# Moving the split activations of a decoder trunk to other byte addresses in SBUF

## The chip, the cores and the metric

The kernel runs on one core of one Trainium2 chip. The metric is the device time of one execution in microseconds. Two timed runs of the kernel before took 1018.0 and 1018.07 us, median 1018.04.

A core has a matrix engine (PE in the profile, with its weight loads shown apart as PEld), a vector engine (DVE), a scalar engine (ACT), a general engine (POOL) and SP, whose queue issues most of the transfers from main memory. Data sits in SBUF, 128 partitions with a byte address along each; products are summed in PSUM, in banks.

## The reference, cut to what matters

A decoder trunk of two layers, 256 positions by 1024 channels, float32. Each layer is a feed-forward block, a token mixer with memory cross-attention beside it, and a second feed-forward block, each added to the residual:

```python
def rms_norm(x, g):
    y = x * lax.rsqrt(jnp.mean(x * x, axis=-1, keepdims=True) + EPS)
    return y * g

def swiglu(x, w_in, w_out):
    gate, up = jnp.split(x @ w_in, 2, axis=-1)
    return (jax.nn.silu(gate) * up) @ w_out

for i in range(2):
    x = x + 0.5 * swiglu(rms_norm(x, ffn1_norm_g[i]), ffn1_w_in[i], ffn1_w_out[i])
    x = x + mixer(rms_norm(x, mix_norm_g[i])) @ w_out      # layer 0: mLSTM, layer 1: windowed attention
    x = x + 0.5 * swiglu(rms_norm(x, ffn2_norm_g[i]), ffn2_w_in[i], ffn2_w_out[i])
```

The hidden width of the feed-forward blocks is 2816. The four feed-forward blocks hold most of the multiplications.

## The kernel before, in words

**Split products.** Every large product is made three times in a rounded float32 format (fp32r). A value is split into a high part (rounded) and a low part (what the rounding left), and the sum high·high + high·low + low·high stands for the full product. `mm3` (L224 to L228) issues these three products: L225 is weights-high by x-high, L226 weights-high by x-low, L227 weights-low by x-high. Each has a stationary operand of 128 by 128, loaded by a weight load of its own, and a moving operand of 128 partitions by 256 columns.

**Weights.** `wtile` (L216) brings a weight tile of 128 by 1024 to the buffer `wr` over SP's queue, and `split` (L204) makes `wh` on ACT (L211) and `wl` on DVE (L212). There are 5, 8 and 8 buffers of these.

**The normed residual.** An object of the class `Norm` stands for each point at which the residual is normed: x0 before the first feed-forward block, x1 before the mLSTM mixer, x2 and x3 before the second and third feed-forward blocks, x4 before the attention mixer, x5 before the last feed-forward block. Its method `put` takes one chunk of the residual at a time (256 channels, `[128, 2, 256]`, four chunks in all), scales it by the norm's gain and splits it (`split_gain`, L239): the high part `xh` by ACT (recorded at L132), the low part `xl` by DVE (L241). The factor of each position (one over the root mean square) is not in there: `chain` (L293) works it out beside the products that already run, with small matrix products on a column of ones (L231) and, a little later, on the identity (also L231, `bcast_rows`), and it is applied to the results.

**A feed-forward block.** `ffn_in` (L471) makes 11 groups of 256 gate and 256 up columns. Each group takes 2 halves of the channels, 2 parts (gate, up), 2 blocks of 128 columns and 4 chunks of 128 channels, three products each: 96. So there are 11 x 96 = 1056 products to a block, in which `xh` or `xl` is the moving operand and `wh` or `wl` the stationary one. The second half of `ffn` (L509) makes the output from the hidden values, which lie in buffers `u`: 22 x 8 x 3 = 528 products with `u` moving. The first product on the last of the four residual chunks is the 55th of a block.

**The mixers.** Some groups of a mixer also have `xh`, `xl` moving; those whose result has positions in rows (`rows=True`) have them stationary and the weights moving. Between these groups stand short products for heads, written in by a planner (`Weave`) with due times.

**Order.** PE and SP run in the order in which the program is written; semaphores are placed by the framework, from what each instruction reads and writes. Tiles come from pools, each with a number of buffers; the pools lie in SBUF in the order in which they are opened (L110 to L125), one behind the other, so the order and the sizes of the pools set the addresses.

**Addresses before.** Taken from the program: `xh` (4 buffers of 2048 bytes) from byte 28608, `xl` from 36800, `u` (31 buffers) from 44992, `v` (2 buffers of 2064 bytes, 2080 apart) from 108480, `wr` from 112640, `wh` from 133120, `wl` from 165888. Counted modulo 512, every `xh`, `xl` and `u` begins at 448, every `wr`, `wh` and `wl` at 0.

Of the kernel before, what the change touches and what calls it, by code (L numbers as in the profile page):

```python
# [11 lines left out]
F32R = mybir.dt.float32r  # L12
# [7 lines left out]
P = 128  # L20
T = 256
# [27 lines left out]
G_MEM, G_F1, G_MIX, G_F2, G_XQ, G_XK, G_AH, G_BQ, G_BK, G_END = 0, 8, 24, 40, 56, 58, 60, 68, 69, 70  # L49
# [6 lines left out]


WARM = 18


class Weave:
# [37 lines left out]
def tile_trunk(ctx: ExitStack, tc: tile.TileContext, a, out):  # L99
# [3 lines left out]
    def mk(pool, shape, dt, tag):  # L103
        seq[0] += 1
        return pool.tile(shape, dt, tag=tag, name=f"{tag}_{seq[0]}")

    def pool(name, bufs, **kw):
        return ctx.enter_context(tc.tile_pool(name=name, bufs=bufs, **kw))

    cst = pool("cst", 1)  # L110
    wv = Weave()


    xhp = pool("xhp", 4)
    xlp = pool("xlp", 4)
    up = pool("up", 31)
    vp = pool("vp", 2)
    wrp = pool("wrp", 5)
    whp = pool("whp", 8)
    wlp = pool("wlp", 8)  # L120
    tp = pool("tp", 7)
    sp = pool("sp", 2)
    ap1 = pool("ap1", 1)
    gp = pool("gp", 1)
    cp = pool("cp", 24)  # L125
# [24 lines left out]
    def mo():  # L150
        return mk(pb8, [P, 512], F32, "bank")
# [47 lines left out]
    def g(i):  # L199
        return gcol[:, i:i + 1]  # L200
# [38 lines left out]
    def split_gain(src, gc, hi, lo):  # L239
        act(hi, src, AF.Copy, scale=gc)  # L240
        nc.vector.scalar_tensor_tensor(out=lo, in0=src, scalar=gc, in1=hi.bitcast(F32),  # L241
                                       op0=ALU.mult, op1=ALU.subtract)
# [18 lines left out]
    class Norm:  # L261


        def __init__(self, gi, rows=True, half=True):
            self.gi, self.rows, self.half, self.rc = gi, rows, half, None
            self.done = False
            self.xT, self.xh, self.xl = [], [], []

        def put(self, xn):
            c2 = len(self.xT)  # L270
            hi, lo = mk(xhp, [P, 2, T], F32R, "xh"), mk(xlp, [P, 2, T], F32R, "xl")
            for m in range(2):
                split_gain(xn[:, m], g(self.gi + 2 * c2 + m), hi[:, m], lo[:, m])
            self.xh.append(hi)
            self.xl.append(lo)
            self.xT.append(xn)
            self.square(xn, c2 == 0)
            if c2 == 3:
                self.fold()
# [115 lines left out]

    kT = [mk(cst, [P, 2, T], F32, f"kT{i}") for i in range(2)]
    vM = mk(cst, [P, 2, 512], F32, "vM")
    x0 = Norm(G_F1)

    def memory():  # L400

# [2 lines left out]
        bank = mo()  # L404
        for i in range(WARM):
            nc.tensor.matmul(bank, idle[:, :P], idle, start=True, stop=True, skip_group_check=True)
# [565 lines left out]

    def program():
        yield from memory()
        x1, x2, x3 = Norm(G_MIX, half=False), Norm(G_F2), Norm(G_F1 + 8)
        x4, x5 = Norm(G_MIX + 8, rows=False), Norm(G_F2 + 8)
        yield from ffn(x0, a["ffn1_w_in"][0], a["ffn1_w_out"][0], x1, late_constants)
        yield from mixer_a(x1, x2)
        yield from ffn(x2, a["ffn2_w_in"][0], a["ffn2_w_out"][0], x3)
        yield from ffn(x3, a["ffn1_w_in"][1], a["ffn1_w_out"][1], x4, rope_tables)  # L980
        yield from mixer_b(x4, x5)
        yield from ffn(x5, a["ffn2_w_in"][1], a["ffn2_w_out"][1])

    with tc.manual_schedule(engines={mybir.EngineType.PE, mybir.EngineType.SP}):
        wv.run(program())
# [38 lines left out]
```

## Time and profile before

| | us |
|---|---|
| median of the two timed runs | 1018.04 |
| the profiled execution | 1018.06 |
| its span, first to last instruction | 1016.3 |
| PE busy | 1007.1 (99%) |
| DVE busy | 656.8 (65%) |
| ACT busy | 520.5 (51%) |

1.8 us of the profiled execution lie outside the span. A product's duration in the trace overlaps the next one's, so the pace of PE is read from the distance between two starts, not from the durations; where a window is asked for, a product counts if any part of it lies inside.

### The profile page before, as it was taken

How to read it: one execution, taken by the hardware profiler on the slowest of the kernel's cores; microseconds unless marked ns; L12 is line 12 of the kernel's file. 1: busy time of each engine (PE TensorE's matmuls, PEld its weight loads, DVE VectorE, ACT ScalarE, POOL GpSimd, SP SyncE). 2: the span in 40 equal slices, each digit the busy share in tenths (PEclk: the TensorE clock that was granted, in tenths of full speed). 3: DMA queues.
4: the chain of work that ended last, by engine and by line, in shares of the span. 5: the costliest groups of instructions: out<-in, count | busy, mean ns of one | idle time of the engine just before them, and what ended most of it. 6: DMA issues, size and time to landing. Idle time of an engine off the chain costs nothing.

```text
span 1016.3 us, 20689 instructions
## 1 busy us (share of the span) xinstructions
PE 1007.1 (99%) x8626; PEld 987.5 (97%) x8626; DVE 656.8 (65%) x1063; ACT 520.5 (51%) x764; POOL 35.5 (3%) x32
## 2 busy tenths in 40 slices
PE   8999999999999999999999999999999999999998
PEld 7999999999999999999999999999978899999998
DVE  6866665567756766665667666555786666665551
ACT  7754545446556644444545444544565654444440
POOL 1200000000000000000000000000211000000000
PEclk9999999999999999999999999999999999999999
DMA  9776655666544476655666666566531256665650
GB/s 311 240 248 194 191 187 182 191 189 180 170 146 145 153 221 192 201 178 187 197 200 195 192 200 190 173 192 204 180 104 63 65 160 214 198 195 179 189 173 21
DMA packets 173204, 182.70 MB, mean 180 GB/s; under 512 B 7124, under 2 KB 168328, under 8 KB 173112
## 3 DMA queue, kind: packets, MB, share of 16 engines
q1 hardware_dynamic: 171872, 179.60, 56.9%
q10 hardware_dynamic: 1016, 1.58, 0.4%
q8 instruction: 67, 1.10, 0.4%
q0 software_dynamic: 224, 0.22, 0.2%
q14 instruction: 25, 0.20, 0.1%
HBM read 180.32 MB, written 1.05 MB: 178 GB/s over the span
## 4 chain that ended last, share of the span: by engine, by line
PE 97%; DVE 1%; DMA 1%; POOL 0%; SPq 0%; ACT 0%; issue 0%
PE bank L225 30%; PE bank L226 30%; PE bank L227 30%; PE bank L231 5%; PE bank L236 1%; DMA wr<-in_mem_w_kv_dram 1%; DVE wl L212 0%; PE bank L921 0%; POOL col L379 0%; DVE col L591 0%; SPq L410 0%; ACT wh L211 0%; DVE u L596 0%; ACT u L132 0%; SPq L218 0%
## 5 line engine op out<-in xcount | busy, mean ns | idle before, releaser
L212 DVE TENSOR_TENSOR wl<-wr,wh 128x1024 fp32r<-128x1024 f32 (+1 forms) x347 | 414.7, 1197 | 280.9 <-ACT wh L211 280.3
L211 ACT CAST wh<-wr 128x1024 fp32r<-128x1024 f32 (+1 forms) x347 | 356.9, 1031 | 396.8 <-PE bank L226 370.7
L225 PE MATMUL bank<-xh,wh 128*128 128x256 f32 x1544 | 429.5, 278 | 0.0
L227 PE MATMUL bank<-xh,wl 128*128 128x256 f32 x1544 | 427.3, 277 | 0.0
L226 PE MATMUL bank<-xl,wh 128*128 128x256 f32 x1544 | 427.3, 277 | 0.0
L226 PEld LDWEIGHTS bank<-xl,wh 128*128 128x128 f32 x1544 | 290.3, 188 | 0.1
L225 PEld LDWEIGHTS bank<-xh,wh 128*128 128x128 f32 x1544 | 290.0, 188 | 0.1
L227 PEld LDWEIGHTS bank<-xh,wl 128*128 128x128 f32 x1544 | 289.9, 188 | 0.0
L225 PE MATMUL bank<-u,wh 128*128 128x256 f32 x896 | 249.2, 278 | 0.0
L227 PE MATMUL bank<-u,wl 128*128 128x256 f32 x896 | 247.9, 277 | 0.0
L226 PE MATMUL bank<-u,wh 128*128 128x256 f32 x896 | 247.9, 277 | 0.0
L225 PEld LDWEIGHTS bank<-u,wh 128*128 128x128 f32 x896 | 168.3, 188 | 0.7 <-issue 0.7
L226 PEld LDWEIGHTS bank<-u,wh 128*128 128x128 f32 x896 | 168.3, 188 | 0.1
L227 PEld LDWEIGHTS bank<-u,wl 128*128 128x128 f32 x896 | 168.3, 188 | 0.0
L225 PE MATMUL bank<-wh,xh 128*128 128x256 f32 x208 | 60.0, 288 | 0.0
L226 PE MATMUL bank<-wl,xh 128*128 128x256 f32 x208 | 58.0, 279 | 0.0
L227 PE MATMUL bank<-wh,xl 128*128 128x256 f32 x208 | 57.9, 278 | 0.0
L476 DVE TENSOR_TENSOR t<-bank,rb 128x256 f32<-128x256 f32 x88 | 36.6, 421 | 7.2 <-PE bank L227 7.2
L225 PEld LDWEIGHTS bank<-wh,xh 128*128 128x128 f32 x208 | 39.1, 188 | 0.5 <-issue 0.3
L226 PEld LDWEIGHTS bank<-wl,xh 128*128 128x128 f32 x208 | 39.1, 188 | 0.1
L227 PEld LDWEIGHTS bank<-wh,xl 128*128 128x128 f32 x208 | 39.0, 188 | 0.0
L479 DVE TENSOR_TENSOR t<-t,bank 128x256 f32<-128x256 f32 x88 | 32.8, 413 | 1.8 <-ACT t L132 1.8
(169 smaller groups left out, 676.0 us busy)
## 6 DMA issues: line engine op xcount, KB each, us to landing
wr<-in_ffn_w_in_dram SPq DMA_DIRECT2D x176, 512.0 KB, 3.7
wr<-in_ffn_w_out_dram SPq DMA_DIRECT2D x80, 512.0 KB, 3.5
wr<-in_a_w_in_dram SPq DMA_DIRECT2D x28, 512.0 KB, 3.7
wr<-in_b_w_in_dram SPq DMA_DIRECT2D x14, 512.0 KB, 4.6
wr<-in_a_w_out_dram SPq DMA_DIRECT2D x12, 512.0 KB, 3.3
wr<-in_b_w_out_dram SPq DMA_DIRECT2D x12, 512.0 KB, 3.3
wr<-in_ffn_w_out_dram SPq DMA_DIRECT2D x16, 256.0 KB, 2.6
wr<-in_mem_w_kv_dram SPq DMA_DIRECT2D x7, 512.0 KB, 8.1
```

What stands on the lines that cost most here:

```text
L211: last[0] = nc.scalar.copy(hi[:, i * n:(i + 1) * n], src[:, i * n:(i + 1) * n])
L212: tt(out=lo[:, i * n:(i + 1) * n], in0=src[:, i * n:(i + 1) * n], in1=hi[:, i * n:(i + 1) * n].bitcast(F32), op=ALU.subtract)
L225: nc.tensor.matmul(ps, wh, xh, start=start, stop=False, skip_group_check=True)
L226: nc.tensor.matmul(ps, wh, xl, start=False, stop=False, skip_group_check=True)
L227: nc.tensor.matmul(ps, wl, xh, start=False, stop=stop, skip_group_check=True)
L231: nc.tensor.matmul(ps, lhsT, rhs, start=start, stop=stop, skip_group_check=True)
L236: nc.tensor.transpose(ps, src, ident[:k, :k])
L476: tt(out=t[:, m], in0=ps[m][:, :T], in1=x.rb, op=ALU.mult)
L479: tt(out=t[:, m], in0=t[:, m], in1=ps[m][:, T:], op=ALU.mult)
```

## The change

The two pools of `xh` and `xl` go. In their place is one pool `xsp` with one buffer of 16 x 256 float32 plus 80: all eight pieces of a `Norm` (four high, then four low) are slices of one tile `xs`. Each `Norm` has an offset `at`, in float32, at which its slices begin: 64 for the two mixers, and 68, 76, 52 and 60 for x0, x2, x3 and x5. The pools `vp` and `sp` are opened earlier, so they move in SBUF too. No instruction is added or taken away by the text of the change, and no product, copy or transfer has another size.

```diff
+XPAD = 80
...
-    xhp = pool("xhp", 4)
-    xlp = pool("xlp", 4)
+    vp = pool("vp", 2)
+
     up = pool("up", 31)
-    vp = pool("vp", 2)
+    sp = pool("sp", 2)
+    xsp = pool("xsp", 1)
     wrp = pool("wrp", 5)
     whp = pool("whp", 8)
     wlp = pool("wlp", 8)
     tp = pool("tp", 7)
-    sp = pool("sp", 2)
...
-        def __init__(self, gi, rows=True, half=True):
-            self.gi, self.rows, self.half, self.rc = gi, rows, half, None
+        def __init__(self, gi, rows=True, half=True, at=64):
+
+            self.gi, self.rows, self.half, self.rc, self.at = gi, rows, half, None, at
...
         def put(self, xn):
             c2 = len(self.xT)
-            hi, lo = mk(xhp, [P, 2, T], F32R, "xh"), mk(xlp, [P, 2, T], F32R, "xl")
+            if c2 == 0:
+                self.tile = mk(xsp, [P, 16 * T + XPAD], F32R, "xs")
+            hi, lo = (self.tile[:, c0:c0 + 2 * T].rearrange("p (m t) -> p m t", m=2)
+                      for c0 in (self.at + 2 * c2 * T, self.at + (8 + 2 * c2) * T))
...
-    x0 = Norm(G_F1)
+    x0 = Norm(G_F1, at=68)
...
-        x1, x2, x3 = Norm(G_MIX, half=False), Norm(G_F2), Norm(G_F1 + 8)
-        x4, x5 = Norm(G_MIX + 8, rows=False), Norm(G_F2 + 8)
+        x1, x2, x3 = Norm(G_MIX, half=False), Norm(G_F2, at=76), Norm(G_F1 + 8, at=52)
+        x4, x5 = Norm(G_MIX + 8, rows=False), Norm(G_F2 + 8, at=60)
```

The change names the phases 464, 496, 400 and 432 in place of 448. That is the position of a slice modulo 512, counted from the position of the weights: 68 is four float32, 16 bytes, behind 64, and so on for +48, -48 and -16 bytes.

## The prediction

> **What bounds the kernel now.** I read the page first, then the pace of PE by windows, then the places where that pace differs. On the page I look at the span, the busy shares, the granted clock and the chain that ended last; of the groups, the three with `xh` or `xl` moving.
>
> ```profile
> span 1016.3 us, 20689 instructions
> ...
> PE 1007.1 (99%) x8626; PEld 987.5 (97%) x8626; DVE 656.8 (65%) x1063; ACT 520.5 (51%) x764; POOL 35.5 (3%) x32
> ...
> PEclk9999999999999999999999999999999999999999
> ...
> PE 97%; DVE 1%; DMA 1%; POOL 0%; SPq 0%; ACT 0%; issue 0%
> ...
> L225 PE MATMUL bank<-xh,wh 128*128 128x256 f32 x1544 | 429.5, 278 | 0.0
> L227 PE MATMUL bank<-xh,wl 128*128 128x256 f32 x1544 | 427.3, 277 | 0.0
> L226 PE MATMUL bank<-xl,wh 128*128 128x256 f32 x1544 | 427.3, 277 | 0.0
> ```
>
> PE is busy for 99% of the span at full clock, and the chain is PE for 97%. No transfer and no other engine is late. So the time is the number of products times their pace, and only the pace, or a new wait on PE, can move it. Of the 3 x 1544 products with x moving, 4 x 1056 = 4224 are in the feed-forward blocks.
>
> The pace, from windows of PE alone (columns: window, its length, busy time with the number of products that touch it, clock, DMA share, GB/s):
>
> ```profile
> 60.00:150.00 90.00, 90.00 (x796) 1.00 0.62 192
> ...
> 375.00:465.00 90.00, 90.00 (x797) 1.00 0.61 191
> 475.00:525.00 50.00, 50.00 (x444) 1.00 0.63 198
> 555.00:645.00 90.00, 90.00 (x797) 1.00 0.63 192
> 655.00:705.00 50.00, 50.00 (x443) 1.00 0.65 197
> 855.00:945.00 90.00, 90.00 (x797) 1.00 0.62 191
> ```
>
> A product that begins up to 0.28 us ahead of a window counts in it, so the pace is (90 + 0.28)/797 = 113.3 ns with x moving, in each block, and (50 + 0.28)/443 or 444 = 113.2 to 113.5 ns with `u` moving. It is one pace for three operand tiles. But there is a second one. At the start of each stage two short groups break the stream: the products on a column of ones and, some microseconds later, those on the identity. The first rows are of the chain of work in order of time (start, length, what), the others of PE in order of time.
>
> ```profile
> 45.81 0.34 PE bank L231 x4
> ...
> 54.73 0.45 PE bank L231 x4
> ...
> 538.36 0.34 PE bank L231 x4
> ...
> 544.46 0.44 PE bank L231 x4
> ...
> 224.03 0.36 PE L225 MATMUL bank<-xh,wh 128*128 128x256 f32 x1
> 224.23 0.28 PE L226 MATMUL bank<-xl,wh 128*128 128x256 f32 x1
> 224.35 0.28 PE L227 MATMUL bank<-xh,wl 128*128 128x256 f32 x1
> ...
> 229.65 0.28 PE L227 MATMUL bank<-xh,wl 128*128 128x256 f32 x1
> 229.77 0.61 PE L231 MATMUL bank<-con,rc 128*128 128x128 f32 x4
> ```
>
> Here 224.35 to 229.65 is 15 rounds of three products: 5.30/45 = 117.8 ns. After the identity products the pace is 113.3 again, with the same tiles at the same addresses. So **PE has two paces, 113.3 and 117.8 ns**, and what sets which one holds, here, is how the stream was last broken. The slow spell lasts 6.1 us in a block (538.36 to 544.46) and 8.9 in the first; three of one and one of the other are 27 us, about 230 of the 4224 products.
>
> The weight load is the nearest limit below. Where a product has one moving column, only loads are left to pace PE:
>
> ```profile
> 223.56 0.53 PEld L231 LDWEIGHTS bank<-ones,acc 128*128 128x128 f32 x4
> 224.00 0.19 PEld L225 LDWEIGHTS bank<-xh,wh 128*128 128x128 f32 x1
> ...
> 357.44 0.52 PEld L231 LDWEIGHTS bank<-ones,acc 128*128 128x128 f32 x4
> 357.89 0.19 PEld L225 LDWEIGHTS bank<-xh,wh 128*128 128x128 f32 x1
> ```
>
> Four loads take 0.44 and 0.45 us from the first start to the next one behind them: 0.89/8 = 111.2 ns. The steady pace is 2.1 ns over that. Loads stay as they are in the feed-forward blocks: there x is the moving operand.
>
> **The change part by part.** *Addresses, by adding pool sizes.* `v` begins at 28608 and takes 2 x 2080, so `u` begins at 32768, which is 0 modulo 512; `sp` takes 4864 bytes, `xs` begins at 101120 and `wr` at 117824, which is 64. With `at` = 64 a mixer's slices begin at 101376, 0 modulo 512: against the weights they lie where they lay, 448 to 0 before and 0 to 64 now, and so does `u`. The four blocks are 16, 48, -48 and -16 bytes off that. So the only products that read from a new place relative to the rest are the 4224; no part of it has a row in this trace, since every x, u and weight slice of before begins at a multiple of 64 bytes.
>
> *What a moving operand off a multiple of 64 costs.* The nearest row is `v`, whose two buffers lie 2080 bytes apart, so every second head reads it 32 bytes off. It moves 257 columns in full float32, two records a product; the first row is of the buffer at a multiple of 64, the second of the other:
>
> ```profile
> 299.55 1.46 PE L231 MATMUL bank<-v,u 128*128 128x257 f32 x6
> ...
> 306.51 1.46 PE L231 MATMUL bank<-v,u 128*128 128x257 f32 x6
> ```
>
> Six records take 1.46 us at both places. At two decimals that is a difference under 0.01/6 = 1.7 ns a record; it is no fp32r stream, which is twice as dense, so it speaks for nothing but doesn't settle it. Bounds for one fp32r product: from below, 111.2 ns, the load alone, -2.1; from above the other pace that the trace shows, 117.8, +4.5. I take 0, because the three operand tiles of before agree within 0.3 ns and the off-line `v` row shows nothing: 4224 x 0 = 0. The ends are 4224 x -2.1 = -8.9 us and (4224 - 230) x 4.5 = +18.0 us.
>
> Two rules of the Trainium skill bear on this. "SBUF — State Buffer", section "Who interferes with whom", gives PE two independent read ports, one for the moving operand and one for weight loads, and says PE never waits on anyone; by it an address can cost nothing and the sum is +0. The trace agrees only in part: by that rule alone no second pace of 117.8 ns would be explained. The same page, "Specifications (TRN2)", has lines of 16 bytes; all four offsets are multiples of 16, so a row of 1024 bytes would touch 64 lines as before, again +0. No run here shows a line's size.
>
> *One tile in place of eight.* It could add a wait if the framework took the tile as a whole: the first product of a block would then wait for the last chunk's split. Rows of PE, ACT and DVE at the start of the first mixer and of the third feed-forward block:
>
> ```profile
> 215.51 0.28 PE L225 MATMUL bank<-xh,wh 128*128 128x256 f32 x1
> ...
> 218.96 0.91 ACT L132 ACTIVATE xh<-u,gcol 128x256 fp32r<-128x256 f32 x2 [2.26 <-DVE u L546]
> ...
> 219.91 0.75 DVE L241 SCALAR_TENSOR_TENSOR xl<-u,gcol,xh 128x256 fp32r<-128x256 f32 x2
> ...
> 530.03 0.28 PE L225 MATMUL bank<-xh,wh 128*128 128x256 f32 x1
> ...
> 535.12 0.88 DVE L241 SCALAR_TENSOR_TENSOR xl<-u,gcol,xh 128x256 fp32r<-128x256 f32 x2
> ```
>
> In program order ACT writes half 0 of the chunk, DVE reads half 0, ACT writes half 1. ACT wrote both by 218.96 + 0.91 = 219.87, ahead of DVE's first read at 219.91, so it didn't wait for a reader of another part of its tile: waits go by the part. I cost it at nothing. The cover is thin, though. The 55th product is the first to need the last chunk: 530.03 + 54 x 0.113 = 536.1, and the split ends at 536.00. A DVE or ACT write that were slower at an odd address by over 0.1 us would show there, tenths of a microsecond for each of five boundaries. The buffer's reuse adds no wait either: a `Norm` is first put some 60 us after the last block's x was read, since `ffn`'s output half lies between, and in a mixer after its last group.
>
> *Weights and transfers* at 64 instead of 0 modulo 512: loads to `u` before went to 448, those to `wr` to 0, and PE hardly waits for either; the five waits of PE that the trace lists are 5.3 us in all, of the view of waits:
>
> ```profile
> PE bank L231 <- ACT u L132: 1.5, 1, 1.5
> PE bank L406 <- DVE t L403: 1.3, 1, 1.3
> PE bank L231 <- ACT t L603: 1.1, 1, 1.1
> PE bank L226 <- DVE wl L212: 0.9, 1, 0.9
> PE bank L225 <- ACT wh L211: 0.5, 1, 0.5
> ```
>
> A slower transfer is covered by five `wr` buffers and DMA engines at 0.62 in the blocks. The sum is 0 on 1018.06, the profiled execution, which stands 0.02 us over the median of the runs: **1018.1 us**.
>
> **The rivals.**
> - *The slow pace holds.* If a shifted moving row meets the weight reads otherwise, a block can stay at 117.8 ns instead of returning to 113.3. For it: the two paces exist for the same tiles, so the stream is sensitive to how reads of the two kinds fall. Against it: in every block of before, the identity products bring 113.3 back. One block costs some 1000 x 4.5 = 4.5 us (1022.6), all four 18 us: 1036. It decides from the first shifted block on; this is the case on the slower side.
> - *A faster pace.* The same sensitivity the other way: the 2.1 ns over the load alone go, 1018.1 - 8.9 = 1009.2 at most. Against it: nothing in the trace runs a 256-column stream under 113.3.
> - *The tile waits as a whole.* PE would stand from a block's first product to the end of the last split: 220.66 - 215.51 = 5.2 us, 536.00 - 530.03 = 6.0 us; five boundaries at 5.6 give 28 us: 1046. Against it is the ACT row above.
>
> **How the numbers follow.** Pace unchanged: 0.53, its own range 1015 to 1021 (the mixers' slow spells may fall otherwise, a few hundred products by 4.5 ns). Slow pace in one to four blocks: 0.23. Faster pace: 0.15. Whole-tile wait: 0.04. A pace worse than either of the two shown: 0.05. The range takes the first three, 1009 to 1036, and leaves out the last two, 0.09. A measurement of this kernel can tell a change from none from about 2%, 998 to 1038. Slower than that are the last two, 0.08 of their 0.09; faster, 0.01; within, 0.91.
>
> **What would show it.** Windows of 90 us inside each block's first part again with 796 or 797 products mean the pace is unchanged; 766 would be 117.8 ns, 811 to 812 would be 111.2. A block that differs from its neighbours would tie the pace to its own offset. A PE idle time at a block's first product, released by DVE `xs`, would mean the whole-tile wait. The prediction is wrong if the pace depends on the moving operand's place within 64 bytes at all.

## The result and the profile after

The changed kernel takes 1041.62 us in the median of two runs (1040.7 and 1042.54) against 1018.04 before: 1.0228 times as long, with a 95% interval of 1.0206 to 1.025. It is slower by 23.6 us, where no change was forecast, and 5.6 us above the end of the range. The profiled execution took 1040.7 us, its span is 1038.9 us, 22.6 over the span of before.

The page of the changed kernel, with its busy times, the granted clock by slices, and the first of the three lines of large products (busy us, mean ns of one, idle time before them):

```profile
span 1038.9 us, 20689 instructions
...
PE 1029.3 (99%) x8626; PEld 1009.9 (97%) x8626; DVE 656.8 (63%) x1063; ACT 519.8 (50%) x764; POOL 33.7 (3%) x32
...
PEclk9999999999999999999999999999999999999999
...
L224 PE MATMUL bank<-xs,wh 128*128 128x256 f32 x1544 | 434.1, 281 | 0.0
```

The number of instructions is the same to the last one. DVE and ACT are busy as long as before. PE is idle for 1038.9 - 1029.3 = 9.6 us, before for 1016.3 - 1007.1 = 9.2: **no new wait**. Of the 22.6 us of span, 22.2 are PE being busy for longer with the same 8626 records of products at the same granted clock. So the loss has to be read from the pace, by windows inside the stages. The columns are the window, its length, PE's busy time with the number of products that touch it, the granted clock, and the DMA share with its GB/s. Odd rows are the first parts of the four feed-forward blocks (x moving), even rows their second parts (`u` moving):

```profile
60.00:150.00 90.00, 90.00 (x774) 1.00 0.60 185
165.00:215.00 50.00, 50.00 (x427) 1.00 0.67 189
375.00:465.00 90.00, 90.00 (x770) 1.00 0.60 186
485.00:535.00 50.00, 50.00 (x444) 1.00 0.64 195
565.00:655.00 90.00, 90.00 (x774) 1.00 0.60 187
670.00:720.00 50.00, 50.00 (x427) 1.00 0.63 189
875.00:965.00 90.00, 90.00 (x757) 1.00 0.59 181
980.00:1030.00 50.00, 50.00 (x444) 1.00 0.41 127
```

A product lasts 0.28 us in the row above, and one that is cut by the window's edge counts; so the pace is (length + 0.28) / count. The first parts run at 116.6, 117.2, 116.6 and 119.3 ns, where before all of them ran at 113.3 or 113.4. The second parts, whose operand `u` lies where it lay against the weights, run at 117.8, 113.2, 117.8 and 113.2: in two of the four the slow one of the two old paces is caught.

The sum, with the prediction's own count of some 998 products in a first part after its opening spell: 998 x (3.3 + 3.9 + 3.3 + 6.0) = 16.5 us, and 2 x 528 x 4.5 = 4.8 us for the second parts of blocks 1 and 3. Both take the pace of the windows as that of the whole part. That is 21.3 of the 22.6 us of span; the other 1.3 lie in the mixers and the opening spells and were not taken apart.

### The profile page after: what moved, and what is told of

Same layout as the page of the kernel before. It is cut to its first block, busy times and chain, and to the rows that moved or that the text cites. A ratio compares the mean times of both kernels' runs of the same rounds, so it can differ in the third digit from the quotient of the medians.

```text
span 1038.9 us, 20689 instructions
## 1 busy us (share of the span) xinstructions
PE 1029.3 (99%) x8626; PEld 1009.9 (97%) x8626; DVE 656.8 (63%) x1063; ACT 519.8 (50%) x764; POOL 33.7 (3%) x32
## 4 chain that ended last, share of the span: by engine, by line
PE 97%; DVE 1%; DMA 1%; POOL 0%; SPq 0%; ACT 0%; issue 0%
PE bank L224 30%; PE bank L225 30%; PE bank L226 30%; PE bank L230 4%; PE bank L235 1%; DMA wr<-in_mem_w_kv_dram 1%; DVE wl L211 0%; PE bank L924 0%; POOL col L382 0%; DVE col L594 0%; SPq L413 0%; ACT wh L210 0%; DVE u L599 0%; ACT u L131 0%; SPq L217 0%
## 5 line engine op out<-in xcount | busy, mean ns | idle before, releaser
L224 PE MATMUL bank<-xs,wh 128*128 128x256 f32 x1544 | 434.1, 281 | 0.0
L225 PE MATMUL bank<-xs,wh 128*128 128x256 f32 x1544 | 432.9, 280 | 0.0
L226 PE MATMUL bank<-xs,wl 128*128 128x256 f32 x1544 | 431.7, 280 | 0.0
L226 PEld LDWEIGHTS bank<-xs,wl 128*128 128x128 f32 x1544 | 291.1, 189 | 0.0
L224 PEld LDWEIGHTS bank<-xs,wh 128*128 128x128 f32 x1544 | 290.6, 188 | 0.1
L225 PEld LDWEIGHTS bank<-xs,wh 128*128 128x128 f32 x1544 | 290.5, 188 | 0.1
L224 PE MATMUL bank<-wh,xs 128*128 128x256 f32 x208 | 60.2, 289 | 0.0
L225 PE MATMUL bank<-wl,xs 128*128 128x256 f32 x208 | 58.1, 279 | 0.0
L226 PE MATMUL bank<-wh,xs 128*128 128x256 f32 x208 | 58.0, 279 | 0.0
L224 PEld LDWEIGHTS bank<-wh,xs 128*128 128x128 f32 x208 | 39.1, 188 | 0.5 <-issue 0.3
L225 PEld LDWEIGHTS bank<-wl,xs 128*128 128x128 f32 x208 | 39.0, 188 | 0.1
L226 PEld LDWEIGHTS bank<-wh,xs 128*128 128x128 f32 x208 | 39.0, 188 | 0.0
```

What stands on the lines that cost most here:

```text
L224: nc.tensor.matmul(ps, wh, xh, start=start, stop=False, skip_group_check=True)
L225: nc.tensor.matmul(ps, wh, xl, start=False, stop=False, skip_group_check=True)
L226: nc.tensor.matmul(ps, wl, xh, start=False, stop=stop, skip_group_check=True)
```

## The experiments

All times are to be held against the kernel before in the same comparison: 1018.26 us for e1 to e4, 1020.25 for e5 to e8, 1018.16 for e9 to e11, 1018.19 for e12. e1 was executed four times; three times lie within 0.6 us, and a fourth, of 2613.02 us, is left out and not explained. The others have one execution each, so the argument goes by the paces in their traces and not by small differences of time. All but e2 are edits of the changed kernel.

Two quantities change together in the kernel after: where x lies within 64 bytes, and how far x lies from the weights. "Distance" below is the address of an x slice minus that of a weight tile, counted modulo 512 (that 256 is enough is a result of the map below). Before it was -64 everywhere; with the change it is -48, -16, -112 and -80 in the four blocks and -64 in the mixers.

### e1_all64: the new tile and pools without the offsets

```diff
-    x0 = Norm(G_F1, at=68)
+    x0 = Norm(G_F1, at=64)
...
-        x1, x2, x3 = Norm(G_MIX, half=False), Norm(G_F2, at=76), Norm(G_F1 + 8, at=52)
-        x4, x5 = Norm(G_MIX + 8, rows=False), Norm(G_F2 + 8, at=60)
+        x1, x2, x3 = Norm(G_MIX, half=False), Norm(G_F2, at=64), Norm(G_F1 + 8, at=64)
+        x4, x5 = Norm(G_MIX + 8, rows=False), Norm(G_F2 + 8, at=64)
```

> One tile and the new pool order stay, but all six norms take the offset 64, so every slice of xs begins at a multiple of 64 bytes. If only the offsets cost (theory A, a moving operand off a 64-byte boundary), all four feed-forward blocks run at 113.3 ns and the time is 1015 to 1021 us. If the shared tile or the moved pools cost (theory T), it stays at 1036 us or more.

Measured: 1024.7 us, 1.006 times the kernel before (1.004 to 1.008). The windows of the first parts of the four blocks, and of the second part of the last:

```profile
60.00:150.00 90.00, 90.00 (x797) 1.00 0.62 191
375.00:465.00 90.00, 90.00 (x796) 1.00 0.62 191
555.00:645.00 90.00, 90.00 (x797) 1.00 0.63 192
860.00:950.00 90.00, 90.00 (x767) 1.00 0.60 183
965.00:1010.00 45.00, 45.00 (x385) 1.00 0.41 124
```

Three blocks are back at 113.3 to 113.4 ns: the shared tile and the moved pools cost nothing there, the offsets do. The last block runs at 117.7 and stays there to its end. Of its 1584 products some 120 come ahead of the group on the identity; the other 1464 by 4.4 ns are 6.4 us, nearly all of the 6.6 us by which the span is longer than before (1022.9 against 1016.3). So the expected time was missed, and for a reason that was not on the list: in that block x, `u` and the weights lie at the same distance as in the other three, and it still holds the slow pace. e8 takes that up.

### e2_eight_tiles: the offsets without the shared tile

The kernel before, with its eight tiles of x, each padded by 128 bytes and its slice shifted inside.

```diff
-            hi, lo = mk(xhp, [P, 2, T], F32R, "xh"), mk(xlp, [P, 2, T], F32R, "xl")
+            hi, lo = (mk(p, [P, 2 * T + 32], F32R, n)[:, self.at:self.at + 2 * T].rearrange("p (m t) -> p m t", m=2)
+                      for p, n in ((xhp, "xh"), (xlp, "xl")))
...
+    x0 = Norm(G_F1, at=20)
...
+        x1, x2, x3 = Norm(G_MIX, half=False), Norm(G_F2, at=28), Norm(G_F1 + 8, at=4)
+        x4, x5 = Norm(G_MIX + 8, rows=False), Norm(G_F2 + 8, at=12)
```

> The kernel before with its own pools and eight separate tiles, each 128 bytes longer, whose slices begin at 464, 496, 400 and 432 modulo 512 for x0, x2, x3, x5 (weights at 0), as far off a 64-byte boundary as in the change. Theory A: the first parts of the four blocks run at 116.7 to 119.3 ns as after the change, and the time is 1036 to 1044 us. Theory T: 1018 us.

Measured: 1040.53 us. The first parts run at 116.9, 118.3, 118.3 and 117.9 ns. Without the shared tile, shifted slices cost about as much, so the tile isn't needed for the loss. It is no clean repeat, though. The offsets count from a buffer that begins at 448, so the slices begin at 16, 48, -48 and -16 bytes from the weights in the four blocks, and not where the expectation puts them. With the padding the buffers lie 2176 bytes apart, so every second chunk lies another 128 bytes on, and the mixers' slices moved too.

### e3_lines and e4_small: is it the place within 64 bytes?

In e3 every x begins at a multiple of 64 bytes again, but at other distances. The longer tile moves the weights as well, to 192 modulo 512, so the distances are -128, -64, -256 and +192.

```diff
-XPAD = 80
+XPAD = 112
...
+    x0 = Norm(G_F1, at=80)
...
+        x1, x2, x3 = Norm(G_MIX, half=False), Norm(G_F2, at=96), Norm(G_F1 + 8, at=48)
+        x4, x5 = Norm(G_MIX + 8, rows=False), Norm(G_F2 + 8, at=32)
```

> The changed kernel with offsets of whole 64 bytes from the place of the mixers: +64, +128, -64 and -128 bytes for x0, x2, x3, x5. Theory A (place within 64 bytes): 113.3 ns in all four, 1015 to 1021 us. Theory R (the distance between moving operand and weights modulo 512 decides, as the change words it): the pace differs from 113.3 ns in at least some blocks, time over 1025 us.

Measured: 1041.04 us. The four first parts, with the second part of the first block behind it:

```profile
65.00:155.00 90.00, 90.00 (x761) 1.00 0.59 183
165.00:215.00 50.00, 50.00 (x427) 1.00 0.65 191
380.00:470.00 90.00, 90.00 (x797) 1.00 0.63 194
570.00:660.00 90.00, 90.00 (x752) 1.00 0.58 179
875.00:965.00 90.00, 90.00 (x796) 1.00 0.62 193
```

That is 118.6, 113.3, 120.1 and 113.4 ns. All four lie at multiples of 64, and two of them pay as much as the shifted blocks did or more: a 64-byte boundary isn't what matters. The two that don't pay are at -64 and at +192, which is -64 modulo 256. The second part, whose `u` stayed while the weights moved, is at 117.8; its distance is now -192, which is +64 modulo 256.

e4 takes smaller steps and odd places: distances -32, -96, -56 and -60.

```diff
+    x0 = Norm(G_F1, at=72)
...
+        x1, x2, x3 = Norm(G_MIX, half=False), Norm(G_F2, at=56), Norm(G_F1 + 8, at=66)
+        x4, x5 = Norm(G_MIX + 8, rows=False), Norm(G_F2 + 8, at=65)
```

> The changed kernel with offsets +32, -32, +8 and +4 bytes for x0, x2, x3, x5. If the boundary is 64 bytes (theory A) all four are over 113.3 ns, by 3 to 6 ns, time 1030 to 1045 us. If it is 32 bytes, x0 and x2 run at 113.3 ns; if it is 16 bytes (a line of 16), +16 of the change would have been free, so that is out already, and x3 and x5 tell whether less than 16 bytes costs more.

Measured: 1048.16 us, the slowest of the shifts and 3 us over what was expected at most. The first parts run at 118.3, 118.8, 120.1 and 121.7 ns; the row of the last one:

```profile
875.00:965.00 90.00, 90.00 (x742) 1.00 0.59 182
```

Four bytes beside the good distance the pace is 121.7 ns, 8.3 over 113.4, the largest loss of all that were tried.

### e6_both32: x and weights moved together

This is the run that decides between the two quantities. x and weights are both shifted by 32 bytes, so neither begins at a multiple of 64, and their distance stays at -64. `u` stays, and comes to lie at -96.

```diff
-XPAD = 80
+XPAD = 88
...
+    x0 = Norm(G_F1, at=72)
...
+        x1, x2, x3 = Norm(G_MIX, half=False, at=72), Norm(G_F2, at=72), Norm(G_F1 + 8, at=72)
+        x4, x5 = Norm(G_MIX + 8, rows=False, at=72), Norm(G_F2 + 8, at=72)
```

> Weights and all slices of x are moved together by 32 bytes, so both are off a 64-byte boundary but their distance is -64 as before; the hidden values u stay where they were, 96 bytes ahead of the weights. Theory R: the first parts of the four blocks run at 113.3 or 117.8 ns, as if nothing were off, and the second parts (u) at another pace, about 118.7. Theory A: the first parts run at 116.7 ns or more, the second at 113.3 or 117.8.

Measured: 1030.26 us. The first part of the first block, its second part, and the first parts of the second and the last block:

```profile
60.00:150.00 90.00, 90.00 (x796) 1.00 0.63 191
160.00:210.00 50.00, 50.00 (x429) 1.00 0.66 191
375.00:465.00 90.00, 90.00 (x797) 1.00 0.62 192
865.00:955.00 90.00, 90.00 (x797) 1.00 0.62 191
```

The first parts, the third block's too, are at 113.3 to 113.4 ns although x lies 32 bytes off a multiple of 64. The second part pays, 117.2 ns, although `u` lies at a multiple of 64 as ever: against it only the weights have moved. So **the pace goes by the distance between the moving and the stationary operand**, and the place of x by itself costs nothing. It is not the distance alone: x at -96 took 118.8 in e4, `u` at -96 takes 117.2, where 118.7 was expected.

The weight buffers are also written, by DMA, ACT and DVE, and these writes moved with them. The end of e6 shows that the pace of `u` there doesn't come from them. There all weights have arrived and been split. The first row gives the busy times of PE, its weight loads, DVE, ACT and POOL, the clock and the DMA share: the last three engines are idle and the DMA share is 0.01. The other two rows are the starts of two products, 17 rounds of three apart:

```profile
1019.00:1024.00 5.00, 5.00 (x45) 5.00 (x44) 0.00 (x0) 0.00 (x0) 0.00 (x0) 1.00 0.01 2
```

```profile
1018.07 0.28 PE L224 MATMUL bank<-u,wh 128*128 128x256 f32 x1
...
1024.05 0.28 PE L224 MATMUL bank<-u,wh 128*128 128x256 f32 x1
```

5.98 us for 51 products are 117.3 ns, the pace of the whole part, with hardly anything at work but PE and its weight loads. The first parts have no such quiet stretch, so for x this wasn't shown apart.

### e5, e9, e10, e11: the map of distances

e5 tries 0, +64, +128 and +192; e9 is the four shifts of the changed kernel dealt to other blocks; e10 has +16, +48, +80 and +112; e11 has +32, +96, -32 and -64.

```diff
 # e5_rel_map
+XPAD = 208
+    x0 = Norm(G_F1, at=80)
+    ... Norm(G_F2, at=96), Norm(G_F1 + 8, at=112) ... Norm(G_F2 + 8, at=128)
 # e9_permuted
+    x0 = Norm(G_F1, at=60)
+    ... Norm(G_F2, at=52), Norm(G_F1 + 8, at=76) ... Norm(G_F2 + 8, at=68)
 # e10_map16
+XPAD = 208
+    x0 = Norm(G_F1, at=84)
+    ... Norm(G_F2, at=92), Norm(G_F1 + 8, at=100) ... Norm(G_F2 + 8, at=108)
 # e11_map32
+XPAD = 208
+    x0 = Norm(G_F1, at=88)
+    ... Norm(G_F2, at=104), Norm(G_F1 + 8, at=72) ... Norm(G_F2 + 8, at=64)
```

> All slices of x begin at multiples of 64 bytes; only the distance from the weights (at 64 modulo 512) is varied: 0, +64, +128, +192 bytes for x0, x2, x3, x5, in place of the -64 of before. Theory R (distance modulo 256 or less decides): x5 (+192 is -64 modulo 256) runs at 113.3 or 117.8 ns, x0 at about 120 and x3 at about 118.7, as -256 and -128 did in the run before; x2 at 117.8 or 113.3 if the period is 128, else something new. Theory A (only the place within 64 bytes): 113.3 or 117.8 in all four.

> The change's own four offsets dealt to other blocks: -80, -112, -16 and -48 bytes from the weights for x0, x2, x3, x5 (offsets 60, 52, 76, 68). If the distance sets the pace (theory R), the paces move with it: 119.3, 116.7, 117.1, 116.7 ns. If block or history sets it, they stay with the blocks: 116.7, 117.1, 116.7, 119.3. Time 1036 to 1046 us.

> Distances +16, +48, +80, +112 bytes for x0, x2, x3, x5, none run before. If the period is 128 bytes they run like -112, -80, -48, -16: 116.7, 119.3, 116.7, 117.1 ns, time 1036 to 1046 us. If it is 256, at least one differs by over 1 ns, and one under 113.3 ns would be worth having.

> Distances +32, +96, -32, -64 bytes for x0, x2, x3, x5. With a period of 128 x0 runs like -96 (118.7 ns) and x2 like -32 (118.3); x3 repeats -32 in another block: 118.3; x5 is at the distance of before: 113.3 or 117.8. A pace under 113.3 ns anywhere would make a version faster than before. Time 1030 to 1042 us.

Measured: 1045.41, 1042.49, 1041.08 and 1039.66 us. The first parts of the four blocks, of e5:

```profile
65.00:155.00 90.00, 90.00 (x752) 1.00 0.59 182
380.00:470.00 90.00, 90.00 (x767) 1.00 0.60 185
570.00:660.00 90.00, 90.00 (x761) 1.00 0.60 184
875.00:965.00 90.00, 90.00 (x767) 1.00 0.59 184
```

of e9:

```profile
65.00:155.00 90.00, 90.00 (x757) 1.00 0.59 182
380.00:470.00 90.00, 90.00 (x774) 1.00 0.60 187
570.00:660.00 90.00, 90.00 (x771) 1.00 0.61 185
875.00:965.00 90.00, 90.00 (x774) 1.00 0.61 186
```

and of the last two blocks of e10:

```profile
570.00:660.00 90.00, 90.00 (x753) 1.00 0.58 179
875.00:965.00 90.00, 90.00 (x797) 1.00 0.62 191
```

e9 is the clearest: its counts 757, 774, 771 and 774 are those of the changed kernel, 757, 774, 770 and 774, in the order of the distances -80, -112, -16 and -48, whichever block has them. A distance has its pace; the block has none of its own.

All the first parts together, in ns per product:

| distance | pace | distance | pace |
|---|---|---|---|
| 0 (e5) and -256 (e3) | 120.1, 120.1 | +128 (e5) and -128 (e3) | 118.6, 118.6 |
| +16 (e10) | 116.6 | -112 (after, e9) | 116.6, 116.6 |
| +32 (e11) | 116.8 | -96 (e4) | 118.8 |
| +48 (e10) | 118.3 | -80 (after, e9) | 119.3, 119.3 |
| +64 (e5) | 117.7 | **-64** (before, e1, e3, e6) | **113.3 or 117.8** |
| +80 (e10) | 119.9 | -60, -56 (e4) | 121.7, 120.1 |
| +96 (e11) | 119.9 | -48 (after, e9) | 116.6, 116.6 |
| **+112** (e10, e12) | **113.3, 113.4** | -32 (e4, e11) | 118.3, 118.3 |
| +192, as -64 (e3, e5) | 113.4 and 117.7 | -16 (after, e9) | 117.2, 117.1 |

0 and -256 agree, +128 and -128 agree, and +192 shows the two paces of -64: a period of 256 bytes fits, 64 does not (0 and -64), and 128 does not (+112 and -16, or +80 and -48). Where -64 stands at 117.7 to 117.8 (the last block of e1 and of e11, +192 in e5) it is the slow one of the two paces that the kernel before has too. None of them is under 113.3, so none of these distances beats the kernel before; only +112 equals it.

### e12_high_low: the high and the low part at distances of their own

```diff
-        def __init__(self, gi, rows=True, half=True, at=64):
+        def __init__(self, gi, rows=True, half=True, at=(64, 64)):
...
-                      for c0 in (self.at + 2 * c2 * T, self.at + (8 + 2 * c2) * T))
+                      for c0 in (self.at[0] + 2 * c2 * T, self.at[1] + 128 + (8 + 2 * c2) * T))
...
+    x0 = Norm(G_F1, at=(64, 108))
...
+        x1, x2, x3 = Norm(G_MIX, half=False), Norm(G_F2, at=(108, 64)), Norm(G_F1 + 8, at=(108, 108))
+        x4, x5 = Norm(G_MIX + 8, rows=False), Norm(G_F2 + 8, at=(64, 128))
```

> High and low parts at distances of their own from the weights, out of those that ran at 113.3 or 113.4 ns before (-64, +112, +192): high -64 and low +112 for x0, high +112 and low -64 for x2, both +112 for x3, high -64 and low +192 for x5. If the distance decides product by product, each block runs at 113.3 to 113.4 ns or, when caught, at 117.8; x3 repeats +112 in another block. If it is the sequence of distances that decides, x0 and x2 have paces of their own, and one under 113.3 ns would beat the kernel before. Time 1016 to 1040 us.

Measured: 1039.64 us. The second and the third block:

```profile
375.00:465.00 90.00, 90.00 (x752) 1.00 0.59 182
570.00:660.00 90.00, 90.00 (x796) 1.00 0.62 191
```

With both parts at +112 the block runs at 113.4, as in e10. With the high part at +112 and the low part at -64, each a distance that by itself can give 113.3, it runs at 120.1; the other way round (first block) at 117.9. So a pace belongs to the sequence of the operands, not to one product. The last block, at -64 and +192, runs at 117.9 too. Its pace and that of the first block are not the same thing, as the times of single products show. These are two lines of the first block (70 to 150 us; busy us, mean ns of one, idle time before them):

```profile
L225 PE MATMUL bank<-xs,wh 128*128 128x256 f32 x228 | 64.5, 283 | 0.0
...
L226 PE MATMUL bank<-xs,wl 128*128 128x256 f32 x227 | 63.0, 278 | 0.0
```

In the last block (885 to 945 us) all three lines have 281, as they have in the last block of e1 on the slow pace. So the last block looks like the slow pace of -64, and the first has a pace of its own.

### e7_wide: does a product with twice the columns hide the loss?

Each product of the first parts moves 512 columns in place of 256 under one weight load; that computes something other than the reference and serves for its pace alone. The distances of the four blocks are -64, -48, -32 and -16.

```diff
-                            mm3(ps[m][:, part * T:(part + 1) * T],
+                            mm3(ps[m],
...
-                                x.xh[kc // 2][:, kc % 2], x.xl[kc // 2][:, kc % 2],
+                                x.xh[kc // 2].rearrange("p m t -> p (m t)"),
+                                x.xl[kc // 2].rearrange("p m t -> p (m t)"),
```

> The products of the first parts move 512 columns (two chunks of 128 channels at once) instead of 256, so the blocks compute something else than the reference; there is one weight load for twice the columns, so the loads are far from the limit. Offsets 0, +16, +32, +48 bytes for x0, x2, x3, x5. If the moving rows themselves are slower to read off a boundary, the pace of x2, x3, x5 is above that of x0 by 3 ns or more. If the loss comes from moving reads and weight reads meeting, with slack between loads it shrinks: all four within 1 ns of each other, near 215 ns. Time about 1450 us either way.

Measured: 1529.1 us. The row of a product on the page (mean 387 ns):

```profile
L224 PE MATMUL bank<-xs,wh 128*128 128x512 f32 (+1 forms) x1544 | 597.1, 387 | 0.0
```

and the windows of the first two blocks' first parts:

```profile
60.00:270.00 210.00, 210.00 (x904) 1.00 0.31 94
480.00:700.00 220.00, 220.00 (x962) 1.00 0.32 97
```

With the length plus 0.39 us over the count, that is 232.7 and 229.1 ns; the other two blocks take 232.2 and 235.7. The expectation fell twice. The paces don't become alike, so one load for twice the columns doesn't remove the dependence on distance; and the shift of 16 bytes is faster than the unshifted row, which a price of the place of x alone can't explain. A product of 512 columns also takes more than two of 256 with a load each, 2 x 113.3 = 226.7.

### e8_breaks: what sets which of the two paces an unshifted block holds

e1, with an extra group of four products on the identity (their result is not used) in the middle of two blocks: in the last one after its second group, in the second one after its fourth and its sixth.

```diff
+            if (x is x5 and gi == 1) or (x is x2 and gi in (3, 5)):
+                bcast_rows(mo(), x.rc)
```

> All offsets 64, as in the first run, where the last block was caught at 117.8 ns from its identity products on. Here four more products on the identity (128 columns, result unused) break the stream: once after the second group of the last block, and after the fourth and the sixth group of the second block. Theory B (each break of this kind moves an aligned stream from one pace to the other, and the pace then holds): the last block goes from 117.8 to 113.3 at its break, the second from 113.3 to 117.8 and back, time 1019 to 1021 us. If breaks don't matter and the last block is slow for another reason, it stays at 117.8 and the time at 1025 us.

Measured: 1022.59 us, 1.6 over the expected range and 2.3 over the kernel before in the same comparison; the paces came as expected. The extra groups in the chain that sets the end (start, us):

```profile
395.83 0.44 PE bank L230 x4
418.89 0.44 PE bank L230 x4
...
858.71 0.44 PE bank L230 x4
```

and windows ahead of them, between them and behind them, three of the second block and one of the last:

```profile
370.00:395.00 25.00, 25.00 (x223) 1.00 0.62 193
397.00:417.00 20.00, 20.00 (x172) 1.00 0.60 183
420.00:470.00 50.00, 50.00 (x444) 1.00 0.61 188
865.00:955.00 90.00, 90.00 (x796) 1.00 0.64 192
```

The second block runs at 113.4 ns, after the first extra group at 117.9, after the second at 113.2. The last block, which ran at 117.7 in e1, runs at 113.4 behind its one extra group; ahead of it, it was on the slow pace here as well (64 products touch the window from 851.0 to 858.3 us, where 113.3 ns would give 66 or 67). At the distance -64 **each such group switches the stream from the one pace to the other, and it then holds until the next break**. A change of operands can switch it too: in the first mixer of the kernel before, 88 products with weights moving (242.0 to 251.7 us) run at 113.4 ns, and the 44 with x moving behind them (252.5 to 257.4 us) at 117.7, with no short group between. The switching also accounts for e1's last block. The window of e1 at the end of the mixer ahead of it, and the two groups that stand between that and the block, on ones and on the identity:

```profile
820.00:839.00 19.00, 19.00 (x164) 1.00 0.46 138
```

```profile
840.29 0.34 PE bank L230 x4
...
846.19 0.44 PE bank L230 x4
```

Its stream came out of the mixer at 19.28 / 164 = 117.6 ns, and two switches leave it where it was, behind the identity at 117.7. The kernel before comes out of the same mixer on the other pace:

```profile
819.00:839.00 20.00, 20.00 (x179) 1.00 0.44 137
```

That is 20.28 / 179 = 113.3, and its last block then ran at 113.4. Why e1 came into the end of the mixer on the slow pace was not followed further back.

## Why the prediction was wrong, step by step

- *What bounds the kernel.* Right: PE sets the end before and after, and the time is the number of products times their pace.
- *Addresses, by adding pool sizes.* Right, and the distances that they gave (unchanged for the mixers and `u`, 16 to 48 bytes off in the four blocks) turned out to be the quantity that matters. The prediction worked them out and then priced another one.
- *What a moving operand off a multiple of 64 costs: "I take 0".* This is the step that failed. Measured were +3.3, +3.9, +3.3 and +6.0 ns for a product, 16.5 us for the four blocks. Its question was wrong as well as its answer: off a multiple of 64 costs nothing (e6), off the distance -64 costs (e3). The `v` row, the evidence for 0, belongs to a full float32 stream, half as dense (1.46/6 = 243 ns a record); the prediction said so, and took it as the nearest row all the same. It was no clean comparison either: `v` has halves of 258 float32 values, so one product in three begins 8 bytes further in both rows. And that three operand tiles agreed within 0.3 ns proved nothing, since all three had the same distance.
- *The upper bound of that step, 117.8 ns.* Too low: block 4 took 119.3, and e4 shows 121.7. The two paces of the trace were no ends of a range; they were the two paces of one distance.
- *The rule of the Trainium skill, "SBUF — State Buffer", section "Who interferes with whom".* By two independent read ports the sum was +0. The runs speak against that sum: with x, `u` and the weights in other places relative to each other, the same products take 113.3 to 121.7 ns. The measurement decides. Whether the two reads themselves delay each other no run shows.
- *Identity products "bring 113.3 back" in every block of before.* The rows were right, the reading was not. The products switch the pace, and ahead of the blocks of before they always met the slow one, which the products on ones had brought (e8, e1). So a pace can be handed on. The sum had no term for products that the change doesn't touch, and these cost 4.8 us: the second parts of blocks 1 and 3, whose distance had not changed, were caught on the slow pace behind first parts at new distances. What decides that isn't known: behind a first part at -80 the second part runs at 113.2 in the last block of the changed kernel and at 117.8 in the first block of e9 (427 products from 165 to 215 us).
- *One tile in place of eight, and weights and transfers.* Right at 0: PE's idle time is 9.6 us against 9.2.
- *The rivals.* "The slow pace holds", with a shifted moving row that "meets the weight reads otherwise", came nearest, at 0.23 with an end of 1036: it had the two operands' places against each other in it, which the runs show to matter, though not how the reads meet; its price went by the two known paces alone and by the first parts alone. The worse pace, 0.05, was left out of the range. The faster pace is excluded for the distances tried.
- *What would show it.* A block that differs from its neighbours was to tie the pace to its own offset, and e9 shows that it does. The last sign, a dependence on "the moving operand's place within 64 bytes", named the wrong quantity: in e6 that place changed and the pace of x did not.

## What to carry to other kernels

Where PE streams products with a weight load each, the order, sizes and padding of SBUF pools are part of its speed: here the distance between the moving and the stationary operand modulo 256 moved the pace by up to 7%, so after any change of layout count the products in a window of each stage, and not only in the stage that was edited. Test a layout by moving both operands together and one alone, which separates a place from a distance. A pace in the trace that holds through one layout is no bound for another, and a stream can inherit its pace from the stage before it, so a step that leaves an operand alone can still change its time.

## What the hardware did that was not expected

The pace depends on the distance between the two operands, with 113.3 ns as the lowest and 121.7 as the highest value seen, on a period that fits 256 bytes, without a simple order between these values (+112 is good, +96 and +80 are among the worst). At one distance there are two stable paces, 113.3 and 117.8, switched by four short products. A product with 512 columns takes 229 to 236 ns, more than two with 256. What inside PE or SBUF makes the pace go by the distance stays open: the traces show starts and counts, not reads. That the slow spells which the kernel before still has (from each group on ones to the one on the identity) could be avoided by breaking the stream elsewhere was not tried.
